# An encoder layer on one core: another sequence of the softmax work, the first norm summed by ScalarE, and a split first load

## The chip, the cores and the metric

The kernel runs on one core of a Trainium2 chip. The metric is the device time of one execution in microseconds (us); the kernel before has a median of 1122.74 us over 3 runs (1122.15 to 1123.06). Profiles and traces are of one execution each. Engines are named PE (TensorE's matrix multiply), PEld (its weight loads, which overlap PE), DVE (VectorE), ACT (ScalarE), POOL (GpSimd) and SP (SyncE, which only issues DMAs here).

## The reference, cut to what matters

One layer over 1024 tokens of width 1024, in float32. What the change touches is the first norm, the input projection and the attention:

```
hn = rmsnorm(h, norm_mix_g[i])
z = hn @ w_in[i]                       # 512 pooling columns, then q, k, v (8 heads of 64)
...
s = jnp.einsum('bqhd,bkhd->bhqk', qb, kb) * scale + bias     # scale 1/8
s = jnp.where(valid[None, None, None, :], s, -jnp.inf)
pr = jax.nn.softmax(s, axis=-1)
return jnp.einsum('bhqk,bkhd->bqhd', pr, vb)
```

Each chunk of 64 queries attends to its own chunk and the 8 before. A pooling mixer, an output projection, a gated MLP with a short convolution, a gated embedding and a last norm follow; the change leaves them alone.

## The kernel before, in words

**Arithmetic.** Every float32 operand of a product is split in two halves of PE's faster float type, hi (a copy, on ACT) and lo (the difference, on DVE). A product is three matmuls: hi by hi, hi by lo, lo by hi (`mm3`, lines 136 to 138). `split` (lines 141 and 142) is the general splitter.

**Start.** Activations lie transposed: rows of `xT` are channels, eight tiles `k` of 128 channels by 1024 tokens. For each `k`, SP's queue brings `xT[k]` in two halves, a tile of `w_v`, and blocks of the first q/k weights `w_qk0`; ACT's queue brings `vecs`, all the per-channel vectors in one, whose first 8 columns are the first norm's. ACT and DVE make hi and lo of x times the norm's vector (lines 248 and 249) and of the weights. PE runs `start_mm(k)` (12 matmuls) and `start_v(k-1)` (9 matmuls). Ahead of all that, 8 matmuls on zeros (line 221) keep PE busy while the first loads come. The norm's 1/rms is applied after the products. For it, `squared(k)` squares `xraw[k]` on ACT (line 227, in place) and adds it to a running sum on DVE (line 229); eight products with a column of ones (line 264) sum over the 128 channels of a tile's rows; DVE and POOL make `rstd_tok` (lines 265 and 266). `rstd_rows` turns it by PE into rows (line 323), between the first `start_v` tiles and the later ones.

**Attention.** A unit is a pair of heads `c` and one or three token tiles (`UNITS`: per pair `(0,1,2)`, then 3, 4, 5, 6, 7; `PER` is 6 and `NU` is 24). `unit(u)` writes for PE: the transposes of the last unit's probabilities (`probs_t`, line 421), this unit's scores (`scores`, line 398), and some steps of the projections still to be made (`fill`, three matmuls a step). At the ends of three groups of tiles, (0,1,2), (3,4,5) and (6,7), `values` (line 473) multiplies the probabilities of the whole group with V. That makes 12 value groups in all, three to each head pair.

The order of PE's work is the program's. In the attention ACT's and DVE's order is written by hand too: each piece of work is pushed with a time in `push(t, ...)`, and `flush()` emits all that is pending, sorted by that time. The pieces of a unit:

- `softmax`: `least` (a fused add and minimum on DVE, lines 363 and 367), the exponentials with their sums (ACT, line 375), the reciprocals (DVE, line 378), and the scaling of the first head of the pair on DVE (line 373) and of the second on ACT (line 371). Scores carry a minus sign: q is scaled by -0.125, and the bias is turned by ACT (`load_bias`, line 351), while POOL writes the masked corners (lines 352 and 353).
- `probs_out`: the transposed probabilities go from PSUM to hi (ACT, line 439) and lo (DVE, line 441). What lies in the banks behind 3 ("far") has later times than the rest ("near"). `values` reads both.
- `lay` (lines 308 to 312) and `split_later` (lines 502 and 504): the halves of q and k for a later unit, and of weights for a later projection. `qk_out` (line 279) and the projection of the pooling columns (line 559) move finished projections out of PSUM.

In `unit`, all that is pending is emitted ahead of the value products. `values` itself ends with two ACT copies into `otmp` (line 476) and two DVE additions (line 479).

Outside the attention a scheduler with a cost model of its own orders ACT, DVE, POOL and the DMA issues; a queue's DMAs are issued one after another.

Of the kernel before, what the change touches and what calls it, by code (L numbers as in the profile page):

```python
# [8 lines left out]
AF = mybir.ActivationFunctionType  # L9
# [89 lines left out]
    return t1 * t + k if t0 == 0 else 5 * (t - t0) + k - t + 4 - max(0, 4 - t0)  # L99


def trunk(tc, xT, pT, vecs, w_qk0, w_in, w_v, bias, counts, pool_w, w_out, w_up, w_down,
          w_gate, w_ple, out):
    nc = tc.nc
    act, dve, pe, pool, sp = nc.scalar, nc.vector, nc.tensor, nc.gpsimd, nc.sync
# [1 line left out]
    with tc.tile_pool(name="sb", bufs=1) as sb, \  # L107
# [42 lines left out]
        pool.memset(ident, 0.0)  # L150
        pool.affine_select(out=ident, in_=ident, compare_op=ALU.not_equal, fill=1.0, base=0,
                           pattern=[[-1, P]], channel_multiplier=1)
        act.activation(small[:, 1:2], mhalf, AF.Exp)
        rstd_tok = small[:, 8:16]
        st = [small[:, b:b + 3] for b in (24, 27, 30, 33, 56, 59, 62, 66)]
        cnt = small[:, 40:56]

# [47 lines left out]
            return PS[:, (4, 5, 6, 4, 5, 6, 7, 3)[t]]  # L205

        def start_mm(k):
            for h in range(2):
                for c in range(2):
                    mm3(PS[:, 2 * c + h], w0h[:, k, c * P:(c + 1) * P], w0l[:, k, c * P:(c + 1) * P],  # L210
                        XTH[h][:, k], XTL[h][:, k], k == 0, k == KT - 1)
# [10 lines left out]

        blocks = {(0, 0): (0, 1), (0, 1): (1, 2), (1, 1): (2, 4), (3, 1): (4, 8)}

        def squared(k):

            act.activation(xraw[k], xraw[k], AF.Square)
            if k:
                dve.tensor_tensor(xraw[0], xraw[0], xraw[k], ALU.add)

        def split_v(k):
            split(wvraw[k % 4], wv[0][:, k], wv[1][:, k])
# [1 line left out]
        for k in range(KT):  # L234
            xs = xraw[k]
            for h in range(2):
                sp.dma_start(xs[:, h * 512:(h + 1) * 512], xT[k, :, h * 512:(h + 1) * 512])
                if k == 0 and h == 0:
                    act.dma_start(vec, vecs)
                if h and k:  # L240
                    sp.dma_start(wvraw[(k - 1) % 4], w_v[:, (k - 1) * 512:k * 512])
                if (k, h) in blocks:
                    ka, ke = blocks[k, h]
                    sp.dma_start(wq[:, ka:ke], w_qk0[:, ka * 256:ke * 256].rearrange("p (k c) -> p k c", c=256))
            g = vec[:, C_GMIX + k:C_GMIX + k + 1]
            for h in range(2):
                xk = xs[:, h * 512:(h + 1) * 512]
                act.activation(XTH[h][:, k], xk, AF.Copy, scale=g)
                dve.scalar_tensor_tensor(XTL[h][:, k], xk, g, rv(XTH[h][:, k]), ALU.mult, ALU.subtract)  # L249
                if h == 0:  # L250
                    split(wq[:, k], w0h[:, k], w0l[:, k])
            if k:
                split_v(k - 1)
                squared(k - 1)
            if k < KT - 1:
                start_mm(k)
            if k:
                start_v(k - 1)
        sp.dma_start(wvraw[(KT - 1) % 4], w_v[:, (KT - 1) * 512:])
        split_v(KT - 1)  # L260
        squared(KT - 1)
        sp.dma_start(cnt, counts)
        for t in range(NTOK):
            pe.matmul(PS[:, 7, t:t + 1], xraw[0][:, t * P:(t + 1) * P], ones, start=True, stop=True)
        dve.tensor_scalar(rstd_tok, PS[:, 7, 0:NTOK], 1.0 / D, EPS, ALU.mult, ALU.add)
        pool.tensor_tensor(rstd_tok, rstd_tok, mhalf.to_broadcast([P, NTOK]), ALU.pow)
        start_mm(KT - 1)
        start_v(KT - 1)
# [12 lines left out]
        laid = set()  # L281
        pending, now, owed = [], [0.0], set()

        def push(t, *fns):

            for n, fn in enumerate(fns):
                pending.append((t + 0.8 * n, len(pending), fn))

        def flush():
            todo = sorted(pending, key=lambda p: p[:2])  # L290
            pending.clear()
            owed.clear()
            for _, _, fn in todo:
                fn()


        def lay(c, x, h):

            z = slice(h * 512, (h + 1) * 512)

            def last(fn):
                fn()
                laid.add((c, x, h))

            src = qk32[x][:, z]
            if x:
# [39 lines left out]
        def load_bias(h):  # L346
            b = biasb[h % 3]
            sp.dma_start(b, bias[h])

            def turned():  # L350
                act.activation(b, b, AF.Copy, scale=-1.0)
                pool.memset(b[0:64, 576:640], BIG)
                pool.memset(b[64:128, 0:64], BIG)
            return turned

        def softmax(todo, valued):

            for i, (x, b, ps, S, s_) in enumerate(todo):
                z = 2 * i / len(todo)

                def least(b=b, ps=ps, S=S, s_=s_):
                    if len(ps.shape) == 3:
                        dve.tensor_tensor_reduce(  # L363
                            S.rearrange("p (a b) -> p a b", a=2), ps,
                            b.rearrange("p (a b) -> p a b", a=2), 1.0, BIG, ALU.add, ALU.min, s_[:, 0:1])
                    else:
                        dve.tensor_tensor_reduce(S, ps, b, 1.0, BIG, ALU.add, ALU.min, s_[:, 0:1])
# [7 lines left out]
                push(1.9 + 0.85 * z, lambda S=S, s_=s_: act.activation(  # L375
                    S, S, AF.Exp, bias=s_[:, 0:1], scale=-1.0, accum_out=s_[:, 1:2]))
# [57 lines left out]
        def probs_out(todo, valued):  # L434
            for a, b, bank, ps in todo:
                src = ps.rearrange("p a (n q) -> p n a q", q=HD)
                hi, lo = [pt[:, a:b].rearrange("p k x (a q) -> p (k x) a q", a=2) for pt in PT]
                far = bank > 3
                push(3.5 if far else 0.0, lambda hi=hi, src=src: act.activation(hi, src, AF.Copy))
                push((3.55 if valued else 4.4) if far else 2.5 if valued else 3.7,  # L440
                     lambda lo=lo, src=src, hi=hi: dve.tensor_tensor(lo, src, rv(hi), ALU.subtract))

        credit, turns, valued = 0.0, [], [False]
# [1 line left out]
        def values(u):  # L445
# [6 lines left out]
            while u < NU - 1 and at[0] < 2.3:  # L452
                next(fill)
                credit -= 0.5
                now[0] += STEP
            flush()
            reach = {k: (max(t0, k), min(t1, k + BANDT)) for k in range(max(0, t0 - 4), t1)}
            wide = [k for k, (a, b) in reach.items() if b - a == n]
            narrow = sorted((k for k in reach if k not in wide), key=lambda k: reach[k][1] - reach[k][0])
# [13 lines left out]
                    pe.matmul(Os[j][:, (a - t0) * P:(b - t0) * P].rearrange("p (t q) -> p t q", q=P), V[:, k, 2 * c_ + j],  # L473
                              PT[part][:, b0:b0 + by * (b - a - 1) + 1:by, j], start=n_ == 0, stop=n_ == len(todo) - 1)
# [22 lines left out]
        def split_later(parts):  # L497

            t = max(5.2, now[0] + 0.4)
            for i, (name, src, hi, lo) in enumerate(parts):  # L500
                def low(name=name, src=src, hi=hi, lo=lo):
                    (pool if name[0] in (4 + 1, 8 + 2, 4 + 2, 8 + 3, 2) else dve).tensor_tensor(lo, src, rv(hi), ALU.subtract)
                    there.add(name)
                push(t + 0.7 * i, lambda src=src, hi=hi: act.activation(hi, src, AF.Copy))
                push(t + 0.8 + 0.7 * i, low)

        def weights(ct, half):

# [138 lines left out]
        def lay_due(u):  # L647

            for c, x, h in list(qk_ready):
                if u >= (c - 1) * PER + (0 if x else PER - 1 if h else 1):  # L650
                    qk_ready.remove((c, x, h))
                    push(max(4.8, now[0] + 0.4), *lay(c, x, h))

        for h in range(3):
            load_bias(h)()
# [1 line left out]
        def unit(u):  # L657
# [758 lines left out]
def _layout(i):  # L1416
# [49 lines left out]
```

## Time and profile before

| what | value |
|---|---|
| median of 3 runs | 1122.74 us (1122.15 to 1123.06) |
| profiled execution | 1122.08 us |
| its span (first to last instruction) | 1120.3 us |
| PE busy | 1108.7 us, 5674 matmuls |
| PEld busy | 921.3 us |
| DVE busy | 850.7 us |
| ACT busy | 581.7 us |
| POOL busy | 167.9 us |
| HBM traffic | 109.13 MB read, 14.68 MB written |

Busy time of an engine is the time that at least one of its instructions was running. Matmuls are pipelined: a 128x512 matmul is shown with 0.39 us, but the next one starts 0.23 us after it, so starts are compared with starts. A row of the timeline gives start, length, engine, line, operation, what is written and read, shape, and the number of instructions merged; the bracket at its end is the engine's idle time just before, and what ended it.

### The profile page before, as it was taken

The page shows a single profiled execution, that of the slowest core. Times are in us where ns is not written, and L with a number is a line of the kernel's source. Part 1 is how long each engine was busy: PE and PEld are TensorE (multiplying, and loading weights), DVE is VectorE, ACT ScalarE, POOL GpSimd, SP SyncE. Part 2 cuts the span into 40 slices and gives each one's busy share as a digit, 9 for nine tenths or more (in the row PEclk, how much of TensorE's full clock was granted, in tenths as well). Part 3 has the DMA queues.
Part 4 walks back from the last instruction along what each step waited for, and adds up shares of the span by engine and source line. Part 5 has one row for each costly group of instructions (what it writes and reads, how often), then busy time and mean ns, then how long its engine had stood idle before and what let it go on. Part 6 is the DMA issues. An engine that isn't in the chain of part 4 may idle for free.

```text
span 1120.3 us, 15614 instructions
## 1 busy us (share of the span) xinstructions
PE 1108.7 (99%) x5674; PEld 921.3 (82%) x5674; DVE 850.7 (76%) x1438; ACT 581.7 (52%) x1006; POOL 167.9 (15%) x212
## 2 busy tenths in 40 slices
PE   9999999999999999999999999999999999999997
PEld 7888888888888888888888888888888888888887
DVE  7537777778578878887787878777877789986845
ACT  8336777765665545443443444344544444674634
POOL 0000101186013200220121012201120112000000
PEclk9999999999999999999999999999999999999999
DMA  8100111104600452764567456756575556420003
GB/s 308 50 1 20 62 43 39 51 16 136 197 29 1 109 155 95 164 156 140 150 160 168 133 160 151 172 138 160 142 174 145 137 156 140 132 94 20 1 34 117
DMA packets 64878, 124.83 MB, mean 111 GB/s; under 512 B 7329, under 2 KB 8737, under 8 KB 64801
## 3 DMA queue, kind: packets, MB, share of 16 engines
q1 hardware_dynamic: 50688, 98.33, 26.8%
q0 software_dynamic: 13824, 25.17, 14.2%
q8 instruction: 44, 0.72, 0.3%
q10 hardware_dynamic: 288, 0.33, 0.1%
q14 instruction: 34, 0.27, 0.1%
HBM read 109.13 MB, written 14.68 MB: 111 GB/s over the span
## 4 chain that ended last, share of the span: by engine, by line
PE 65%; DVE 3%; issue 2%; ACT 1%; POOL 1%; POOLq 0%; DVEq 0%; ACTq 0%
PE PS L136 21%; PE PS L137 21%; PE PS L138 21%; DVE R L142 1%; ACT R L141 1%; POOL TB L925 0%; POOL F L915 0%; DVE F L907 0%; DVE F L1191 0%; ACT TB L896 0%; PE PS L778 0%; POOL small L782 0%; ACT F L770 0%; DVE TB L918 0%; DVE TB L919 0%
## 5 line engine op out<-in xcount | busy, mean ns | idle before, releaser
L136 PE MATMUL PS<-R 128*128 128x512 f32 (+1 forms) x1088 | 422.2, 388 | 0.2
L137 PE MATMUL PS<-R 128*128 128x512 f32 (+1 forms) x1088 | 418.7, 385 | 0.0
L138 PE MATMUL PS<-R 128*128 128x512 f32 (+1 forms) x1088 | 418.5, 385 | 0.0
L136 PEld LDWEIGHTS PS<-R 128*128 128x128 f32 x1088 | 204.6, 188 | 44.6 <-issue 2.9
L138 PEld LDWEIGHTS PS<-R 128*128 128x128 f32 x1088 | 204.5, 188 | 41.3
L137 PEld LDWEIGHTS PS<-R 128*128 128x128 f32 x1088 | 204.6, 188 | 39.8 <-DVE R L249 0.2
L141 ACT ACTIVATE R<-F 128x512 fp32r<-128x512 f32 (+2 forms) x221 | 137.4, 636 | 177.1 <-PE PS L137 85.6
L142 DVE TENSOR_TENSOR R<-F,R 128x512 fp32r<-128x512 f32 (+2 forms) x221 | 154.5, 713 | 49.7 <-ACT R L141 49.0
L1160 DVE TENSOR_TENSOR F<-F,PS 128x512 f32<-128x512 f32 x140 | 92.6, 681 | 6.8 <-PE PS L138 6.5
L850 DVE TENSOR_TENSOR F<-F 128x512 f32<-128x512 f32 x88 | 60.5, 688 | 44.8 <-DMA F<-in_w_up 42.1
L141 ACT ACTIVATE BQ<-RW 128x512 fp32r<-128x512 f32 x90 | 52.6, 622 | 80.4 <-PE PS L137 76.3
L1103 POOL DMA_DIRECT2D RW<-Yd x56 | 49.5, 889 | 264.4 <-DMA RW<-Yd 200.8
L1103 POOL DMA_DIRECT2D RW<-in_w_down x40 | 36.5, 966 | 228.7 <-DMA RW<-in_w_down 191.1
L142 DVE TENSOR_TENSOR BQ<-RW,BQ 128x512 fp32r<-128x512 f32 x90 | 59.1, 684 | 2.6 <-PE PS L137 2.2
L137 PE MATMUL PS<-BQ 128*128 128x512 f32 x140 | 54.6, 390 | 0.1
L136 PE MATMUL PS<-R,BQ 128*128 128x512 f32 x140 | 54.5, 389 | 0.0
L138 PE MATMUL PS<-R,BQ 128*128 128x512 f32 x140 | 54.5, 389 | 0.0
L136 PE MATMUL PS<-BQ 128*128 128x512 f32 x140 | 54.5, 389 | 0.0
L137 PE MATMUL PS<-R,BQ 128*128 128x512 f32 x140 | 54.5, 389 | 0.0
L138 PE MATMUL PS<-BQ 128*128 128x512 f32 x140 | 54.5, 389 | 0.0
L986 ACT ACTIVATE F<-F,vec 128x1024 f32<-128x1024 f32 (+1 forms) x25 | 28.6, 1143 | 44.1 <-DVE F L961 41.9
L375 ACT ACTIVATE F<-F,small 128x640 f32<-128x640 f32 (+4 forms) x64 | 44.0, 689 | 14.0 <-DVE small L363 12.6
(177 smaller groups left out, 1589.7 us busy)
## 6 DMA issues: line engine op xcount, KB each, us to landing
F<-in_w_up SPq DMA_DIRECT2D x91, 256.0 KB, 4.3
RW<-Yd SPq DMA_DIRECT2D x60, 256.0 KB, 3.8
RW<-Yd POOLq DMA_DIRECT2D x56, 256.0 KB, 4.9
RW<-in_w_down SPq DMA_DIRECT2D x50, 256.0 KB, 2.9
RW<-in_w_down POOLq DMA_DIRECT2D x40, 256.0 KB, 6.6
Yd<-F SPq DMA_DIRECT2D x40, 256.0 KB, 3.1
F<-in_w_in SPq DMA_DIRECT2D x10, 512.0 KB, 3.5
F<-in_xT SPq DMA_DIRECT2D x16, 256.0 KB, 5.4
```

Source lines behind the costliest of these rows:

```text
L136: pe.matmul(ps, ahi, bhi, start=first, stop=False, skip_group_check=more)
L137: pe.matmul(ps, ahi, blo, start=False, stop=False, skip_group_check=more)
L138: pe.matmul(ps, alo, bhi, start=False, stop=last, skip_group_check=more)
L141: both = (act.activation(hi, src, AF.Copy), dve.tensor_tensor(lo, src, rv(hi), ALU.subtract))
L142: dve.tensor_tensor(lo, src, rv(hi), ALU.subtract))
L375: push(1.9 + 0.85 * z, lambda S=S, s_=s_: act.activation(S, S, AF.Exp, bias=s_[:, 0:1], scale=-1.0, accum_out=s_[:, 1:2]))
L850: return dve.tensor_tensor(rawu[to], rawu[a], rawu[b], op)
L986: act.activation(y, Gb[:, 2 + a:2 + b], AF.Identity, bias=vec[:, C_CB + fi:C_CB + fi + 1], scale=cw(2))
L1103: pool.dma_start(t, src, accum_op=ALU.add)
L1160: dve.tensor_tensor(t, t, PS[:, 4 + d], ALU.subtract if n in (1, 5) else ALU.add)
```

## The change

- **Order of the attention's work.** `push` takes a mark `slow`, which `lay_due` and `split_later` set. Ahead of a value group only what is not slow is emitted, then the value products; the slow pieces are emitted after the first half's copy and addition (groups of three tiles), or after both (the group of two). The copies and additions at the end of `values` now alternate. In `probs_out`, the far hi copy has time 0.05 in place of 3.5, and the far lo difference directly follows the near one, which has 3.55 in place of 3.7 where no value group follows.
- **Sign of the scores.** q is scaled by +0.125; `least` multiplies by -1 in the same instruction. ACT's turning of the bias goes; the two masked corners are written by DVE with -BIG in place of POOL with BIG.
- **The norm's sums.** A second copy of the input, `xn`, lies token by token. Its eight tiles of 128 tokens by 1024 channels (512 KB each) are loaded by SP into the `xraw` buffers after use, the first four inside the loop over `k`, the others after it. ACT squares each in two halves and sums along the row in the same instruction (`accum_out`). The running sum on DVE and the eight products with ones on PE go.
- **The first loads.** ACT's queue brings only the first norm's 8 columns of `vecs`, then the second half of `xT[0]`; then comes the `Exp` that had stood at the top of ACT's stream. The rest of `vecs` follows on SP's queue. The hi of the first q/k weight tile is a DVE copy in place of ACT's, and `start_mm(0)` has another order: per half of the tokens, hi by hi for both weight columns, then lo by hi, then hi by lo.

```diff
-        act.activation(small[:, 1:2], mhalf, AF.Exp)
...
+            if k == 0:
+                for h in range(2):
+                    for i, (w_, x_) in enumerate(((w0h, XTH), (w0l, XTH), (w0h, XTL))):
+                        for c in range(2):
+                            pe.matmul(PS[:, 2 * c + h], w_[:, 0, c * P:(c + 1) * P], x_[h][:, 0], start=i == 0, stop=False)
+                return
...
-            act.activation(xraw[k], xraw[k], AF.Square)
-            if k:
-                dve.tensor_tensor(xraw[0], xraw[0], xraw[k], ALU.add)
+            for h, s in enumerate((rstd_tok, ssq2)):
+                half = xraw[t][:, 512 * h:512 * (h + 1)]
+                act.activation(half, half, AF.Square, accum_out=s[:, t:t + 1])
+
+        def load_tokens(t):
+            sp.dma_start(xraw[t], xn[t])
...
-                    act.dma_start(vec, vecs)
+                    act.dma_start(vec[:, 0:C_CW], vecs[:, 0:C_CW])
+                    act.dma_start(xs[:, 512:1024], xT[0, :, 512:1024])
+                    act.activation(small[:, 1:2], mhalf, AF.Exp)
+                if (k, h) == (1, 1):
+                    sp.dma_start(vec[:, C_CW:], vecs[:, C_CW:])
...
+                if h == 0 and k == 0:
+                    dve.tensor_copy(w0h[:, 0], wq[:, 0])
+                    dve.tensor_tensor(w0l[:, 0], wq[:, 0], rv(w0h[:, 0]), ALU.subtract)
...
-                squared(k - 1)
+            if k > 3:
+                load_tokens(k - 4)
+            if k > 4:
+                squared(k - 5)
...
-        squared(KT - 1)
+        for t in range(4, NTOK):
+            load_tokens(t)
+        for t in range(3, NTOK):
+            squared(t)
         sp.dma_start(cnt, counts)
-        for t in range(NTOK):
-            pe.matmul(PS[:, 7, t:t + 1], xraw[0][:, t * P:(t + 1) * P], ones, start=True, stop=True)
-        dve.tensor_scalar(rstd_tok, PS[:, 7, 0:NTOK], 1.0 / D, EPS, ALU.mult, ALU.add)
+        dve.tensor_tensor(rstd_tok, rstd_tok, ssq2, ALU.add)
+        dve.tensor_scalar(rstd_tok, rstd_tok, 1.0 / D, EPS, ALU.mult, ALU.add)
...
-        def flush():
-            todo = sorted(pending, key=lambda p: p[:2])
-            pending.clear()
+        def flush(part=False):
+            todo = sorted((p for p in pending if not (part and p[3])), key=lambda p: p[:2])
+            pending[:] = [p for p in pending if part and p[3]]
...
-            return [lambda: act.activation(hi, src, AF.Copy, scale=-0.125),
-                    lambda: last(lambda: dve.scalar_tensor_tensor(lo, src, -0.125, rv(hi), ALU.mult, ALU.subtract))]
+            return [lambda: act.activation(hi, src, AF.Copy, scale=0.125),
+                    lambda: last(lambda: dve.scalar_tensor_tensor(lo, src, 0.125, rv(hi), ALU.mult, ALU.subtract))]
...
-                act.activation(b, b, AF.Copy, scale=-1.0)
-                pool.memset(b[0:64, 576:640], BIG)
-                pool.memset(b[64:128, 0:64], BIG)
+                dve.memset(b[0:64, 576:640], -BIG)
+                dve.memset(b[64:128, 0:64], -BIG)
...
-                        dve.tensor_tensor_reduce(S, ps, b, 1.0, BIG, ALU.add, ALU.min, s_[:, 0:1])
+                        dve.tensor_tensor_reduce(S, ps, b, -1.0, BIG, ALU.add, ALU.min, s_[:, 0:1])
...
-                push(3.5 if far else 0.0, lambda hi=hi, src=src: act.activation(hi, src, AF.Copy))
-                push((3.55 if valued else 4.4) if far else 2.5 if valued else 3.7,
+                push(0.05 if far else 0.0, lambda hi=hi, src=src: act.activation(hi, src, AF.Copy))
+                push((2.5 if valued else 3.55) + 0.02 * far,
...
-            flush()
+            flush(True)
...
-                act.activation(otmp[halves[j], 0:n * P], Os[j][halves[1 - j]], AF.Copy)
-            for j in range(2):
                 a = halves[j]
-                dve.tensor_tensor(o32[a, c_, t0 * P:t1 * P], Os[j][a], otmp[a, 0:n * P], ALU.add)
+                act.activation(otmp[a, 0:n * P], Os[j][halves[1 - j]], AF.Copy)
+                if n == 2 and j == 0:
+                    continue
+                for i in range(2) if n == 2 else (j,):
+                    a = halves[i]
+                    dve.tensor_tensor(o32[a, c_, t0 * P:t1 * P], Os[i][a], otmp[a, 0:n * P], ALU.add)
+                if j == 0:
+                    flush()
...
+            if valued[0]:
+                flush(True)
+                values(u - 1)
             flush()
-            if u:
-                values(u - 1)
...
+    d["xn"] = c(x).reshape(NTOK, P, D)
```

More of the change, by code (lines that the diff above doesn't have):

```diff
@@ L99, in block_at, with trunk @@
     return t1 * t + k if t0 == 0 else 5 * (t - t0) + k - t + 4 - max(0, 4 - t0)
-def trunk(tc, xT, pT, vecs, w_qk0, w_in, w_v, bias, counts, pool_w, w_out, w_up, w_down,
+def trunk(tc, xT, xn, pT, vecs, w_qk0, w_in, w_v, bias, counts, pool_w, w_out, w_up, w_down,
           w_gate, w_ple, out):
@@ L152, in trunk @@
                            pattern=[[-1, P]], channel_multiplier=1)
-        act.activation(small[:, 1:2], mhalf, AF.Exp)
-        rstd_tok = small[:, 8:16]
+        rstd_tok, ssq2 = small[:, 8:16], small[:, 56:64]
         st = [small[:, b:b + 3] for b in (24, 27, 30, 33, 56, 59, 62, 66)]
@@ L223, in trunk, with squared @@
         blocks = {(0, 0): (0, 1), (0, 1): (1, 2), (1, 1): (2, 4), (3, 1): (4, 8)}
-        def squared(k):
-            act.activation(xraw[k], xraw[k], AF.Square)
-            if k:
-                dve.tensor_tensor(xraw[0], xraw[0], xraw[k], ALU.add)
+        def squared(t):
+            for h, s in enumerate((rstd_tok, ssq2)):
[3 more added lines that the diff above has]
+            sp.dma_start(xraw[t], xn[t])
         def split_v(k):
@@ L236, in trunk @@
             for h in range(2):
-                sp.dma_start(xs[:, h * 512:(h + 1) * 512], xT[k, :, h * 512:(h + 1) * 512])
+                if (k, h) != (0, 1):
+                    sp.dma_start(xs[:, h * 512:(h + 1) * 512], xT[k, :, h * 512:(h + 1) * 512])
                 if k == 0 and h == 0:
-                    act.dma_start(vec, vecs)
+                    act.dma_start(vec[:, 0:C_CW], vecs[:, 0:C_CW])
[3 more added lines that the diff above has]
+                    sp.dma_start(vec[:, C_CW:], vecs[:, C_CW:])
                 if h and k:
@@ L249, in trunk @@
                 dve.scalar_tensor_tensor(XTL[h][:, k], xk, g, rv(XTH[h][:, k]), ALU.mult, ALU.subtract)
-                if h == 0:
+                if h == 0 and k == 0:
+                    dve.tensor_copy(w0h[:, 0], wq[:, 0])
+                    dve.tensor_tensor(w0l[:, 0], wq[:, 0], rv(w0h[:, 0]), ALU.subtract)
+                elif h == 0:
                     split(wq[:, k], w0h[:, k], w0l[:, k])
@@ L282, in trunk, with push @@
         pending, now, owed = [], [0.0], set()
-        def push(t, *fns):
+        def push(t, *fns, slow=False):
             for n, fn in enumerate(fns):
-                pending.append((t + 0.8 * n, len(pending), fn))
-        def flush():
-            todo = sorted(pending, key=lambda p: p[:2])
-            pending.clear()
+                pending.append((t + 0.8 * n, len(pending), fn, slow))
+        def flush(part=False):
+            todo = sorted((p for p in pending if not (part and p[3])), key=lambda p: p[:2])
+            pending[:] = [p for p in pending if part and p[3]]
             owed.clear()
-            for _, _, fn in todo:
-                fn()
+            for p in todo:
+                p[2]()
         def lay(c, x, h):
@@ L364, in least @@
                             S.rearrange("p (a b) -> p a b", a=2), ps,
-                            b.rearrange("p (a b) -> p a b", a=2), 1.0, BIG, ALU.add, ALU.min, s_[:, 0:1])
+                            b.rearrange("p (a b) -> p a b", a=2), -1.0, BIG, ALU.add, ALU.min, s_[:, 0:1])
                     else:
-                        dve.tensor_tensor_reduce(S, ps, b, 1.0, BIG, ALU.add, ALU.min, s_[:, 0:1])
+                        dve.tensor_tensor_reduce(S, ps, b, -1.0, BIG, ALU.add, ALU.min, s_[:, 0:1])
                 def scaled(x=x, S=S, s_=s_):
@@ L503, in low @@
                     there.add(name)
-                push(t + 0.7 * i, lambda src=src, hi=hi: act.activation(hi, src, AF.Copy))
-                push(t + 0.8 + 0.7 * i, low)
+                push(t + 0.7 * i, lambda src=src, hi=hi: act.activation(hi, src, AF.Copy), slow=True)
+                push(t + 0.8 + 0.7 * i, low, slow=True)
         def weights(ct, half):
@@ L651, in lay_due @@
                     qk_ready.remove((c, x, h))
-                    push(max(4.8, now[0] + 0.4), *lay(c, x, h))
+                    push(max(4.8, now[0] + 0.4), *lay(c, x, h), slow=True)
         for h in range(3):
```

## The prediction

> **What bounds the kernel now.** I read the page first, then PE's waits, then PE's timeline around them, then the other engines there.
>
> ```profile
> span 1120.3 us, 15614 instructions
> PE 1108.7 (99%) x5674; PEld 921.3 (82%) x5674; DVE 850.7 (76%) x1438; ACT 581.7 (52%) x1006; POOL 167.9 (15%) x212
> ```
> PE is the bound. An edit pays where it removes PE instructions or a stall of PE, and nowhere else. PE's waits from 44 to 330 us, the stretch that holds the attention:
>
> ```profile
> PE PS L473 <- DVE B L441: 1.8, 4, 0.8
> PE PS L421 <- DVE B L441: 0.8, 2, 0.5
> PE PS L473 <- ACT B L439: 0.5, 1, 0.5
> ```
> Columns: waiter and awaited; total, times, longest. All seven waits are for hi (439) or lo (441) of the probabilities. Idle time understates them, since a busy PE may be draining, so I compare equal stretches. PE's timeline, value products (473) and transposes (421):
>
> ```profile
> 104.06 1.33 PE L473 MATMUL PS<-B,R 128*128 128x384 f32 x7
> 105.68 2.70 PE L473 MATMUL PS<-B,R 128*128 128x128 f32 x17 [0.29 <-DVE B L441]
> ...
> 119.92 0.51 PE L473 MATMUL PS<-B,R 128*128 128x256 f32 x3
> 120.97 0.96 PE L473 MATMUL PS<-B,R 128*128 128x128 f32 x6 [0.55 <-ACT B L439]
> 122.39 2.02 PE L473 MATMUL PS<-B,R 128*128 128x128 f32 x15 [0.46 <-DVE B L441]
> ...
> 149.07 3.66 PE L473 MATMUL PS<-B,R 128*128 128x384 f32 x24
> ...
> 159.04 0.92 PE L421 MATMUL PS<-ident,F 64*128 64x64 f32 x20 [0.33 <-DVE B L441]
> ...
> 166.78 2.96 PE L473 MATMUL PS<-B,R 128*128 128x256 f32 x24
> ...
> 176.90 1.79 PE L473 MATMUL PS<-B,R 128*128 128x384 f32 x12
> ...
> 219.18 0.73 PE L473 MATMUL PS<-B,R 128*128 128x384 f32 x4
> 220.67 1.31 PE L473 MATMUL PS<-B,R 128*128 128x128 f32 x8 [0.76 <-DVE B L441]
> ...
> 249.65 0.59 PE L421 MATMUL PS<-ident,F 64*128 64x64 f32 x12 [0.46 <-DVE B L441]
> ```
> Group (3,4,5): 104.06 to 108.38 is 4.32 us, its twin at 149.07 takes 3.66, so the stall costs 0.66. The first row of waits has four, 1.8 us in all; less 0.29, 0.46 and 0.76 a fourth of 0.29 is left, a like group: 0.66 again. Group (6,7): 119.92 to 124.41 is 4.49 against 2.96: 1.53. Group (0,1,2): 219.18 to 221.98 is 2.80 against 1.79: 1.01. For the two stalled transposes I take the idle time, 0.33 and 0.46. Together 2 x 0.66 + 1.53 + 1.01 + 0.79 = 4.65 us. That is all the order of ACT and DVE can return.
>
> **The change, part 1: the order in the attention.** What was late in each stall:
>
> ```profile
> 105.20 0.42 DVE L441 TENSOR_TENSOR B<-PS,B 128x256 fp32r<-128x256 f32 x1
> ...
> 117.64 0.29 DVE L367 CUSTOM_DVE_ANT_0 F<-PS,F 128x128 f32<-128x128 f32 x1 [1.07 <-POOL F L352]
> ...
> 157.19 0.67 DVE L279 TENSOR_TENSOR F<-PS,F 128x512 f32<-128x512 f32 x1
> 157.77 1.54 DVE L441 TENSOR_TENSOR B<-PS,B 128x1024 fp32r<-128x1024 f32 x2
> ```
> The far lo stood behind reciprocals and a scaling; now it directly follows the near lo. At 105.20 the near one (1.21 us, as the 183.02 row below) had been done since about 104.6, so the far one ends near 105.0, and the eighth product, free at about 105.2 (104.06 + 1.33 less a drain), finds it. That stall and its like go. At 119.92 the far hi, behind six exponentials, released PE at 120.97, and the far lo at 122.39. With time 0.05 the far hi precedes the exponentials. Also `least` no longer waits 1.07 us for POOL's corner, since DVE writes it in its own order; near lo (1.21) and far lo (0.42) then end some 2.2 us sooner, near 120.1, while hi products still occupy PE. Both stalls go. At 157.19 an evacuation due at 3.6 stood ahead of a near lo due at 3.7, and before 249.65 one stood ahead of a far lo due at 4.4; 3.55 and 3.57 now precede them, and PE gets its bank 0.67 us sooner, more than 0.33 and 0.46. The evacuations come up to 1.54 us later; no PE row waits on line 279 or 559, so I price that at nothing. At 219 the far lo moves ahead of a scaling: gone too.
>
> What the change adds: the deferred halves (`lay`, weights) now run between the two `otmp` copies, ahead of the next unit's `least`.
>
> ```profile
> 176.92 0.62 ACT L504 ACTIVATE R<-F 128x512 fp32r<-128x512 f32 x1
> ...
> 180.31 0.82 DVE L363 CUSTOM_DVE_ANT_0 F<-PS,F 128x640 f32<-128x640 f32 x1 [0.50 <-PE PS L398]
> ...
> 183.02 1.21 DVE L441 TENSOR_TENSOR B<-PS,B 128x1024 fp32r<-128x1024 f32 x1
> ...
> 184.51 0.84 PE L421 MATMUL PS<-ident,F 64*128 64x64 f32 x20
> ```
> This is the fullest group, (0,1,2) of the third pair: three deferred ACT copies of 0.62 us, and DVE differences after them. They now stand between the copies of the two halves, 1.86 us in a place where PE's second half (0.9, half of 1.79) had ACT idle for perhaps 0.4: the second addition comes 1.4 later. Less the 0.50 idle ahead of `least`, plus two corners of 0.1 (estimate: a quarter of the 0.42 for 128x256), `least` starts 1.1 later, at 181.4. The near lo ends at 185.3 in place of 184.2, and the transposes, which came at 184.51, wait 0.8. The like group of the second pair has two deferred copies and gets perhaps 0.1. In the group of two the deferred work follows both copies and delays the next unit's start by a copy, 0.6; that eats perhaps 0.3 of the return at 219, where the scaling is now last. I take 1.2 us lost. Bounds: 0, if ACT's and DVE's idle time swallows it; 2.2, if four groups lose 0.55. Part 1 nets 4.65 - 1.2 = 3.45 (2.4 to 4.65).
>
> ACT also loses eight turnings of the bias and DVE gains 16 corners: both engines have idle time around (0.50 in the `least` row), so beyond the stalls named nothing.
>
> **Part 2: the sums of the first norm.** PE loses the products with ones.
>
> ```profile
> 39.37 1.84 PE L264 MATMUL PS<-small,F 128*128 128x1 f32 x16
> 41.07 0.49 PE L136 MATMUL PS<-R 128*128 128x512 f32 x1
> ...
> L227 ACT ACTIVATE F<-F 128x1024 f32<-128x1024 f32 x8 | 8.4, 1046 | 0.0
> L375 ACT ACTIVATION_READ_ACCUMULATOR F<-F,small 128x1 f32 x64 | 12.0, 187 | 0.0
> 10.00:20.00 10.00, 10.00 (x46) 8.23 (x45) 9.99 (x17) 10.00 (x18) 0.00 (x0) 1.00 1.04 391
> 19.92 0.33 SPq L259 DMA_DIRECT2D F<-in_w_v  x1
> F<-in_w_v SPq DMA_DIRECT2D x8, 256.0 KB, 5.5
> 41.57 1.67 POOL L266 TENSOR_TENSOR small<-small 128x8 f32<-128x8 f32 x1 [5.54 <-DVE small L265]
> 45.98 0.60 PE L323 MATMUL PS<-ident,small 128*128 128x128 f32 x4
> ```
> 41.07 - 39.37 = 1.70 us leave PE's stream, which is full there: a certain gain. What it costs lies beside PE. DVE loses seven additions; ACT's 8.4 us become 16 halves of 0.523 + 0.187 = 11.4 us. SP's queue gains 4.19 MB while the window row shows 16 full DMA engines (share 1.04) at 391 GB/s: 10.7 us more of transfers. The last weight tile, issued at 19.92, lands about 25.4, so the last tokens land by about 36.1. Two halves (1.4), two DVE steps on 128x8 (0.4 at most, the price of 128x256) and POOL's 1.67 follow: `rstd_tok` by about 39.7. PE's turning into rows needs it at 45.98, now 2.0 sooner, at 44.0; the spare is 4 us. The products with ones had no other user. x and the weights behind the token tiles (up to three tiles, 4 us, before `xT[7]`) are used far later than they land: `xT[7]` only from 41.07, now 39.1. Bias and projection weights behind them come 11 us later, for use after 70 us. So nothing.
>
> **Part 3: the first loads.**
>
> ```profile
> 1.49 3.78 PE L221 MATMUL PS<-B 128*128 128x512 f32 x8 [1.49 <-DVE B L219]
> 5.31 0.80 PE L136 MATMUL PS<-R 128*128 128x512 f32 x1
> ...
> 6.68 0.39 PE L136 MATMUL PS<-R 128*128 128x512 f32 x1
> ...
> 4.23 0.72 ACT L248 ACTIVATE R<-F,vec 128x512 fp32r<-128x512 f32 x1 [1.56 <-DMA vec<-in_vecs]
> vec<-in_vecs ACTq DMA_DIRECT2D x1, 68.0 KB, 3.5
> small<-in_counts SPq DMA_DIRECT2D x1, 8.0 KB, 4.4
> ```
> ACT's queue issues the small vector and x's second half while ACT idles (1.56 us in the 4.23 row); the rest of `vecs`, 64 KB, costs SP's stream 0.2 us at 391 GB/s ahead of the first `w_v` tile, whose products come only after the 24 of `start_mm(0)` and `start_mm(1)`. The eight zero matmuls end at 5.27, and the first real one starts at 5.31: little can be won before it. Behind it three starts are late for their operands, 5.31 to 6.68 where full rate would take 3 x 0.23; at most 0.7 us. The new order asks for the lo halves later, but these matmuls also run slowly: eight in 3.78 us is (3.78 - 0.80) / 7 = 0.43 a step against 0.23 after 6.68. Four at 0.43 from 5.1 put the fifth near 6.8, against 6.91 now. I take 0.3. Bounds: 0.7 gained if the rate is full from 5.3, 0.9 lost if the small first vector lands as late as the small `counts` does (4.4 against 3.5).
>
> [...]
>
> **Sum.** 3.45 + 1.70 + 0.3 = 5.45 us. The profiled execution's 1122.08 (span 1120.3 and 1.8 around it) becomes 1116.6; it stands 0.66 below the median, from which the sum gives 1117.3. I say 1117.0. Behind 250 us PE has no wait in its view, so an earlier start moves everything up.
>
> **The rivals.**
> - *The wait moves to the transposes* (chance 0.18): what the far lo and the deferred work push back, scaling and the next near lo, becomes what PE waits for in most groups. For: the 184.51 calculation. Against: the scaling has a whole value group (1.8 to 3.7 us) before it is read. Then half of Part 1's net: 5.45 - 1.7 = 3.7, 1119.0.
> - *The deferred halves delay `least` everywhere; slower* (0.07): the place is the unit after each of the 12 value groups, the price up to one 0.62 copy and one 0.69 difference, 1.3 us. It decides when the mean loss passes (4.65 + 2.0) / 12 = 0.55 us; at 0.8 the time is 1122.7 + 2.9 = 1125.6. Against: only the fullest groups have more than one deferred copy.
> - *The norm comes late* (0.08): if ACT or SP put the bias and weights first, `rstd_tok` comes past 44.0 and PE idles. Each us beyond costs one; past 5.45 the change is no gain. With 4 us: 1121.
> - *The start gains nothing, the clock's doing* (0.05): half rate past 6.7 us hides the operands' lateness; the sum without the 0.3 is 1117.3. [...]
>
> **How the numbers follow.** The forecast, with most stalls gone and one or two small new ones, has 0.62. A measurement here tells 0.2%, 2.2 us, from no change. The forecast, the last rival and the first are faster: 0.85; of these I leave 0.03 to gains below 2.2. Same: that 0.03 and most of the late norm, 0.09. Slower: the second rival and the worst of the third, 0.09. The range: below, all of Part 1 and 0.7 from Part 3 give 7.05, 1115.0 from the profiled execution; above, the first rival with Part 1 at its low bound and 0.9 lost at the start, 1122.7 - 2.4 / 2 - 1.7 + 0.9 = 1120.7. Outside lie the slower rival, half of the late norm, and a few hundredths of the forecast.
>
> **What would show it.** Line 264 gone from PE and 1.7 us with it. In PE's waits the three rows gone or under 1 us, and the value groups at 1.8, 3.0 and 3.7 us each. A wait of some 0.7 us at the transposes after the third pair's first group. The fifth real matmul near 6.7. POOL's power ending before 40, and PE not waiting for it. I am wrong if PE waits anew on the scalings (371, 373), on a deferred half, or at the rows of `rstd_tok`.

## The result, and the profile after: 6 us slower

The changed kernel has a median of 1128.51 us (1126.68 to 1130.56), the kernel before on the same chip 1122.16: ratio 1.0054, 95% interval 1.0041 to 1.0067. The forecast was 1117.0, faster. The profiled execution took 1126.68 us. Head of its page:

```profile
span 1124.9 us, 15599 instructions
PE 1109.0 (99%) x5658; PEld 919.9 (82%) x5658; DVE 842.8 (75%) x1449; ACT 579.9 (52%) x1021; POOL 163.5 (15%) x196
```

The profiled execution is the fastest of the six; it is 4.6 us longer than that of before (1122.08), so of the 6 us some 1.4 lie outside what this trace shows.

PE issues 16 matmuls fewer and is busy no shorter. PE's waits from 44 to 330 us, in the form of the three rows of before (transposes are now line 441, scores 418, value products 493, hi 459, lo 461, pushed weights 529 and 527):

```profile
PE PS L441 <- DVE B L461: 3.9, 7, 0.8
PE PS L136 <- ACT B L529: 1.5, 1, 1.5
PE PS L493 <- ACT F L391: 0.9, 1, 0.9
PE PS L138 <- DVE B L527: 0.3, 1, 0.3
PE PS L493 <- DVE B L461: 0.2, 1, 0.2
```

The value products' waits for hi and lo are down from 2.3 us to 0.2. That is idle time, which understates a stall: the first row below shows none and is 0.44 us longer than the second. By the lengths of the twelve value groups, the prediction's own measure, less is gained: together they take 37.7 us before and 36.2 here (sums of such rows). Two rows for the first pair's group (3,4,5), the first from after, the second from kernel e10 below, where nothing holds it up:

```profile
102.62 4.09 PE L493 MATMUL PS<-B,R 128*128 128x384 f32 x24
```
```profile
101.98 3.65 PE L493 MATMUL PS<-B,R 128*128 128x384 f32 x24
```

It took 4.32 before (prediction). So stalls of the value products remain, and the transposes now wait seven times for the lo (3.9 us). PE also waits for pieces of weights at lines 136 and 138, where it waited for nothing. The wait of 0.9 is put down to ACT's scaling (391, in the group at 167.02). The evacuation in line 300 ended 0.05 us before that scaling, and in e1 and e5 the same place waits for line 300, so the trace leaves open which of the two PE needed.

PE's timeline dates the loss; with the rows of before at 41.07, 184.51 and 220.67 (prediction) each start gives a shift:

```profile
38.58 0.39 PE L136 MATMUL PS<-R 128*128 128x512 f32 x1
...
97.98 0.92 PE L441 MATMUL PS<-ident,F 64*128 64x64 f32 x20 [0.62 <-DVE B L461]
...
143.09 0.92 PE L441 MATMUL PS<-ident,F 64*128 64x64 f32 x20 [0.84 <-DVE B L461]
...
185.73 0.83 PE L441 MATMUL PS<-ident,F 64*128 64x64 f32 x20 [0.83 <-DVE B L461]
...
221.86 1.68 PE L493 MATMUL PS<-B,R 128*128 128x128 f32 x8 [0.16 <-DVE B L461]
...
263.30 0.50 PE L136 MATMUL PS<-R,B 128*128 128x512 f32 x1 [1.51 <-ACT B L529]
...
264.35 0.50 PE L138 MATMUL PS<-R,B 128*128 128x512 f32 x1 [0.32 <-DVE B L527]
```

38.58 against 41.07: the start gained 2.5 us in this trace (part of that is the clock, see Part 3 below). 185.73 against 184.51 and 221.86 against 220.67: by then the attention has given back 3.7. The same matmul as at 263.30 started at 259.24 before: the last 2.9 us go between 221 and 263. From there on nothing changes (4.7 late at the end). So the whole loss of this trace lies in the attention.

What made the lo late is in DVE's waits, 72 to 262 us, after:

```profile
DVE F L502 <- ACT F L497: 19.8, 17, 4.0
DVE F L383 <- ACT B L459: 19.6, 16, 3.0
```

The first row, the additions behind the `otmp` copies, was 19.0 us before and is little changed. `least` (363 before, 383 now) waits 16 times for ACT's hi copy, 19.6 us. The same stretch of before has `least` wait for the scores:

```profile
DVE F L363 <- PE PS L398: 12.2, 13, 2.3
```

In the timeline of after, ACT, then DVE, in one unit:

```profile
137.80 1.28 ACT L459 ACTIVATE B<-PS 128x1024 fp32r<-128x1024 f32 x2
...
139.12 0.82 DVE L383 CUSTOM_DVE_ANT_0 F<-PS,F 128x640 f32<-128x640 f32 x1 [1.01 <-ACT B L459]
```

The two hi copies, near and far, end at 139.08, and `least` starts 0.04 behind them, having idled 1.01 us. In the same unit of before, `least` ran beside the near copy:

```profile
139.24 1.01 ACT L439 ACTIVATE B<-PS 128x1024 fp32r<-128x1024 f32 x1
```
```profile
139.63 0.82 DVE L363 CUSTOM_DVE_ANT_0 F<-PS,F 128x640 f32<-128x640 f32 x1
```

So it is the far copy that holds `least`. By the code, the scores lie in banks 4 to 7 of PSUM (the memory for PE's results), and the far probabilities in the last columns of banks 6 and 7; the near ones lie in 2 and 3. So `least` and the far copy read the same two banks, in other columns, and neither uses what the other makes. With time 0.05 the far copy comes first in the program, and in the rows of after `least` starts only when it is done (139.12 against 139.08). What makes it wait no run shows; the traces show the waits and that they follow the program's order. With the copy second, in kernel e1 below, it is ACT's copy that waits, three times, for a `least` (line 387):

```profile
ACT B L459 <- DVE small L387: 2.9, 3, 1.0
```

### The profile page after: what moved, and what is told of

It reads as the page before. It is cut to its first block, busy times and chain, and to the rows that moved or that the text cites. A ratio compares the mean times of both kernels' runs of the same rounds, so it can differ in the third digit from the quotient of the medians.

```text
span 1124.9 us, 15599 instructions
## 1 busy us (share of the span) xinstructions
PE 1109.0 (99%) x5658; PEld 919.9 (82%) x5658; DVE 842.8 (75%) x1449; ACT 579.9 (52%) x1021; POOL 163.5 (15%) x196
## 4 chain that ended last, share of the span: by engine, by line
PE 84%; DVE 7%; ACT 5%; issue 3%; POOL 1%; POOLq 0%; DVEq 0%; ACTq 0%
PE PS L136 26%; PE PS L137 26%; PE PS L138 26%; PE PS L493 3%; ACT F L395 2%; DVE B L461 2%; ACT B L459 1%; DVE F L383 1%; DVE R L142 1%; PE PS L441 1%; PE PS L418 1%; ACT R L141 0%; POOL TB L951 0%; POOL F L941 0%; ACT F L497 0%
```

## The experiments

Two theories. **A**: the far hi copy, now ahead of `least` on the same banks, delays `least`, the exponentials and the near lo in the units that have a far part. **B**: the deferred pieces (`slow`) do it. Each kernel's ratio is to the kernel before on the same chip; us in the text are ratio differences times 1122.5. The 95% interval of a ratio is 1 to 2 us to either side, and a difference of two is uncertain by as much.

**e1, undo A.** After, with

```diff
-                push(0.05 if far else 0.0, lambda hi=hi, ...
+                push(2.4 if far else 0.0, lambda hi=hi, ...
```

> The kernel after, with one number changed: the far hi copy has time 2.4 in place of 0.05, so that ACT's copy is emitted after both `least` of its unit, and still ahead of the far lo. Theory A (readers of one PSUM bank are ordered: `least` reads banks that the far hi copy reads too, and with the copy emitted first it waits for ACT): the 19.6 us that line 383 waited for ACT's line 459 in the kernel after go, and the transposes no longer wait for the near lo in units without deferred work; some 5 us come back, about 1123.5 from 1128.5. Theory B (the deferred halves make the loss): no more than 1 us changes, 1127.5 to 1129.

1123.28 us, ratio 1.0003 (0.9994 to 1.0012): 5.7 us of the loss gone, as A said. PE's waits:

```profile
PE PS L136 <- ACT B L529: 1.5, 1, 1.5
PE PS L441 <- DVE B L461: 1.2, 2, 0.8
PE PS L493 <- DVE F L300: 0.9, 1, 0.9
PE PS L138 <- DVE B L527: 0.3, 1, 0.3
```

The transposes' waits fall from 3.9 to 1.2; what B names (529, 527) stays. On DVE, 72 to 262 us, the 19.6 us that `least` waited for ACT's copy are gone, and it waits for the scores again:

```profile
DVE F L383 <- PE PS L418: 10.2, 9, 2.2
```

**e2, A alone.** Before, with far hi at 0.05 in place of 3.5 and nothing else.

> The kernel before, with one number changed: the far hi copy has time 0.05 in place of 3.5, nothing else of the change. Theory A: `least` starts behind ACT's copy in every unit with a far part, 0.7 to 0.9 us later, and PE waits at the transposes: 4 to 6 us slower than before, 1126 to 1128. Theory B: nothing lost, and the stall of 1.5 us at the first group of two partly gone: 1121 to 1122.5.

1129.66, ratio 1.0067 (1.005 to 1.0084): 7.5 us lost by one number, more than the 4 to 6 expected. DVE's waits, 72 to 262 us, and PE's, 44 to 330:

```profile
DVE F L363 <- ACT B L439: 19.8, 16, 3.1
```
```profile
PE PS L473 <- DVE B L441: 4.6, 7, 1.5
PE PS L421 <- DVE B L441: 2.4, 4, 0.7
```

The same 16 waits on DVE, and PE's waits go from 3.1 us to 7.0. A is shown from both sides.

**e3, undo B.** After, all pieces again emitted at one flush ahead of the value products:

```diff
-            if valued[0]:
-                flush(True)
-                values(u - 1)
             flush()
+            if u:
+                values(u - 1)
...
-            flush(True)
+            flush()
```

> The kernel after, without the deferral: all that is pending is emitted ahead of the value products, as before; the far hi copy keeps its early time. Theory A: the losses of the units with deferred work go (2.2 us at the first projection matmul after the last value products, 1.0 and 0.5 at the transposes after the first groups of the third and second pair), the rest stays: about 1124.5. Theory B: most of the loss goes, 1119 to 1121.

1123.81, ratio 1.0014 (1.0004 to 1.0023): 4.5 us of the loss gone, while `least` still waits 16 times for ACT's copy (19.9 us). So A is not the only cause.

**e5, undo both.**

> The changed kernel with the far hi copy at time 2.4 (behind the least of its unit) and without the deferral (every pushed piece runs at the first flush, values ahead of it as before). Theory A (same-bank order holds least up) and theory B (deferred halves) are separate causes: their shares 5.2 and 4.7 us add, 1128.5 - 9.9 = 1118.6, which is 1.4 below the kernel with the start alone (1120.0); that 1.4 is then what the rest of the attention's part (near lo ahead of evacuations, DVE's corners) is worth. Rival: both put off the same chain (least, exponentials, near lo), so that either one alone leaves it just off PE's path; then undoing the second adds little, 1122 to 1123.

1119.37, ratio 0.9971 (0.996 to 0.9982): 9.3 us faster than after, where the two separate shares add to 10.2. They are separate causes, and the rival (either alone suffices) falls. PE's remaining waits:

```profile
PE PS L493 <- DVE F L300: 0.9, 1, 0.9
PE PS L418 <- DVE F L502: 0.9, 2, 0.5
```

**e7, B alone**: before, with the deferral and the alternating copies only.

> The kernel before with only the deferral and the alternating otmp copies and additions of the value groups; far hi stays at 3.5, the start and the signs as before. Theory B: 1125.5 to 1127.5, 3 to 5 us slower than before, 1.8 to 2.2 of it a wait of PE behind the last value products, for the last unit's weight halves (ACT and DVE). Theory A as the only cause: the same as before, 1122 to 1123.

1127.82, ratio 1.0045 (1.003 to 1.006): 5.0 us lost. **e8, B without the last unit**: after, with

```diff
-                flush(True)
+                flush(u < NU)
```

> The changed kernel, with the deferral left out in the last unit only. Theory B at its largest single place: the 1.5 us wait for ACT's weight half and the 0.3 to 0.5 us for DVE's behind it are gone, 1.8 to 2.2 us; if the drop of the granted clock that followed that wait in one profile also comes often, another 0 to 1.7: 1124.6 to 1126.7, with a narrower spread than 1126.7 to 1130.6. If the wait only moves to another operand of those matmuls: 1128, as changed.

1125.28, ratio 1.0025 (1.0014 to 1.0035): 3.3 us better than after; the waits for 529 and 527 are gone from its list and nothing comes in their place. So 3.3 of B's 4.5 us lie in this one place. The timeline of after, ACT and then DVE, shows why:

```profile
261.82 0.77 ACT L497 ACTIVATE F<-PS 64x256 f32<-64x256 f32 x2 [3.03 <-PE PS L493]
262.62 0.63 ACT L529 ACTIVATE B<-F 128x512 fp32r<-128x512 f32 x1
```
```profile
263.51 0.78 DVE L527 TENSOR_TENSOR B<-F,B 128x512 fp32r<-128x512 f32 x1
```

After the last group PE's next work is a projection with that weight, not another unit's transposes. Before, the same difference ran ahead of the last value products:

```profile
255.35 0.68 DVE L502 TENSOR_TENSOR B<-F,B 128x512 fp32r<-128x512 f32 x1
```

Deferred, it stands behind them, while ACT idles 3.03 us. The rest of B is in the groups of three tiles, as in e7's timeline, ACT and then DVE:

```profile
223.54 0.49 ACT L477 ACTIVATE F<-PS 64x384 f32<-64x384 f32 x1 [1.37 <-PE PS L473]
223.93 0.62 ACT L509 ACTIVATE R<-F 128x512 fp32r<-128x512 f32 x1
224.57 0.48 ACT L477 ACTIVATE F<-PS 64x384 f32<-64x384 f32 x1
```
```profile
224.06 0.55 DVE L482 TENSOR_TENSOR F<-PS,F 64x384 f32<-64x384 f32 x1 [1.11 <-ACT F L477]
224.58 1.02 DVE L507 TENSOR_TENSOR R<-F,R 128x512 fp32r<-128x512 f32 x1
225.63 0.56 DVE L482 TENSOR_TENSOR F<-PS,F 64x384 f32<-64x384 f32 x1
```

ACT idles 1.37 us for the products, and then does the weight between the two copies; the second addition, which frees the bank, starts at 225.63, where without the weight's copy on ACT and its difference on DVE it could follow the first at about 224.6 (an estimate: 224.06 + 0.55).

**e4 and e12, the start.** Before with parts 2 and 3 alone (e4), and with the norm's sums alone (e12).

> The kernel before with the two start parts of the change alone: the norm's sums on ScalarE from token tiles, and the first loads with the new order of the first matmuls. Sequence and sign of the attention are those of before. Both theories place the loss in the attention, so this one keeps what the trace of the kernel after shows ahead of it: PE reaches the first scores 2.6 us sooner, 1119.5. If the start were part of the loss (its DMAs or its later weights), 1122 or more.

> The kernel before with the norm's sums alone (token tiles, squares summed by ACT, no products with ones); first loads as before. The prediction's step: 1.70 us of PE's stream gone, nothing waits: 1121.1, ratio 0.9985. With the measured gain of sums and first loads together, 2.5, the first loads are then worth 0.8. Rival: the norm's row products come to wait; then a wait of PE for POOL shows near 44 us, and the gain is smaller.

e4: 1120.01, ratio 0.9978 (0.9969 to 0.9988), 2.5 us gained; e12: 1120.94, ratio 0.9985 (0.9976 to 0.9994), 1.7 us, which leaves 0.8 for the first loads. e12's list of PE's waits is that of before, row for row.

**e6, far hi behind the exponentials where a unit has six `least`.** Both undone, and there far hi 3.4, far lo 3.45.

> As the kernel with both undone, but in the units of three token tiles, which have six least, the far hi has time 3.4 and the far lo 3.45; elsewhere 2.4 and 2.52. Theory A: where there are six least, a far hi at 2.4 still stands in ACT's queue ahead of two or three exponentials and waits there for the last least of its bank; putting it behind them takes away the wait of the value products for the evacuation (0.9 us once with the far hi at 2.4): 0.5 to 1.5 us faster than with both undone. If the far hi's place past the last least does not matter: the same within 0.4.

1119.27, ratio 0.997 (0.9958 to 0.9981): the same as e5, and the wait of the value products for the evacuation (line 300) stays at 0.9. So that the far hi stands ahead of some exponentials is not the cause of this wait.

**e9 to e11**, each with both undone and one thing more: corners by POOL and ACT as before (e9); near lo at 3.7 again where no value group follows (e10); the second weight halves sooner (e11).

> As the kernel with both undone (1119.4, ratio 0.9971 to the kernel before), but the bias is again turned by ACT and its corners are written by POOL. The prediction's step: DVE's corners take POOL's 1.07 us out of least's way, and cost nothing else; then this is up to 1 us slower than with both undone, and the product group of two stalls again (ratio about 0.998). Rival: DVE's two corners (0.11 us each, 0.3 with their gaps, right ahead of least) cost as much as POOL's did: the same within 0.4, and the 0.9 us wait of the value products for the evacuation shrinks to about 0.6.

> As the kernel with both undone, but in the units without value products of a group the near lo has time 3.7 again, behind an evacuation due at 3.6. The prediction's step: the evacuation behind the near lo costs nothing, and the near lo behind the evacuation costs 0.33 to 0.79; then 0.3 to 0.8 us slower. Rival: the later evacuation delays the laid halves, the next least and so the next evacuation, which held the value products for 0.9 us once; then that wait goes, and this is the same or up to 0.6 faster.

> As the kernel with both undone, but ACT's copy of a weight tile's second half has time 3.85 or the time of its request, ahead of the scalings (ACT waits there for reciprocals, 1.2 us in one case), where it had 5.2 or later, ahead of the copies of the value products. If the scores' two waits of 0.4 to 0.5 us come from that copy standing ahead of the otmp copies: they go, 0.5 to 1.2 us faster (about 1118.4). If the copy then delays ACT's scaling, or the halves are not the ones in the way: the same within 0.4.

e9: 1119.35, ratio 0.9969 (0.9958 to 0.9981): who writes the corners makes no difference that can be measured. e11: 1119.31, ratio 0.9967 (0.9955 to 0.998): no difference either, and it decides little, because in its trace the copies at the two places of the scores' waits had not moved.

e10: 1117.98, ratio 0.9957 (0.9945 to 0.997), the lowest of all: its highest run, 1118.78, is under the lowest of e9 on the same chip, 1118.86. The rival of the expectation was right about the direction; the gain, 1.3 to 1.6 us against e9, e11 and e5, is more than its 0.6. e5's timeline, DVE and then ACT:

```profile
154.92 1.54 DVE L461 TENSOR_TENSOR B<-PS,B 128x1024 fp32r<-128x1024 f32 x2
156.37 0.68 DVE L300 TENSOR_TENSOR F<-PS,F 128x512 f32<-128x512 f32 x1
157.75 0.69 DVE L333 SCALAR_TENSOR_TENSOR R<-F,R 128x512 fp32r<-128x512 f32 x1 [0.70 <-ACT R L332]
```
```profile
157.09 0.63 ACT L332 ACTIVATE R<-F 128x512 fp32r<-128x512 f32 x1 [1.22 <-DVE F L300]
```

The evacuation (300) behind the near lo makes ACT wait 1.22 us for it in `lay`, and DVE then 0.70 for ACT; that comes off the next unit's `least`, and at that unit's end an evacuation again is late for the value products (it starts at 164.19 in e5 and at 162.78 in e10; 0.6 of the difference comes from the start of the kernel). In e10:

```profile
154.89 1.54 DVE L461 TENSOR_TENSOR B<-PS,B 128x1024 fp32r<-128x1024 f32 x2
156.35 0.68 DVE L333 SCALAR_TENSOR_TENSOR R<-F,R 128x512 fp32r<-128x512 f32 x1
```

Line 333 follows at once, and PE's list has no wait for line 300 left:

```profile
PE PS L418 <- DVE F L502: 0.9, 2, 0.5
PE PS L441 <- DVE B L461: 0.6, 1, 0.6
```

e10 is the change without three of its steps. It beats both kernels, and the median forecast for the whole change, 1117.0, lies 1.0 below it.

## Why the prediction was wrong, step by step

By the runs: start -2.5; the attention's other edits -2.4 (e10 against e4); near lo ahead of the evacuation +1.6 (e10 to e5); far hi early +5.7 (e1); deferral +4.5 (e3). That sums to +6.9; the last two overlap by 0.9 (e5), which leaves the measured +6.0. The small shares (1.6, and the overlap of 0.9) are no larger than their uncertainty.

- **The step that failed most: "With time 0.05 the far hi precedes the exponentials."** I counted what the far hi gains on ACT and not what it is moved past: `least`, on DVE, which reads the same banks. Price 5.7 us (7.5 in e2, alone), given as nothing. Neither the sum nor a rival had it. The first rival named the place, the transposes, but by scalings and deferred work and at 1119.0; the slower rival had `least` late everywhere, but by the deferred pieces, and at 1125.6.
- **Deferral: 1.2 us lost, 2.2 at most; measured 4.5 (e3) and 5.0 (e7).** For the third pair's first group the place and size were right: a wait of 0.8 was forecast at 184.51, and the transposes there wait 0.83, in after and in e1 alike (0.8, the longest of its two). What was missed is the last unit, 3.3 us by e8. I priced the group of two as delaying "the next unit's start", and the last group has no next unit: PE needs the deferred weight there at once. The 1.2 us that are left of the 4.5 equal the forecast, but only one of its places was compared with a row, so part of that may be luck. A wait of PE on a deferred half, which the prediction named as a sign that it is wrong, is in after's list (529 and 527).
- **"The evacuations come up to 1.54 us later; no PE row waits on line 279 or 559, so I price that at nothing."** Wrong by 1.6 us. Line 279 was off PE's list because it came in time; behind it stand `lay`, the next `least` and the next evacuation. The 0.33 and 0.46 that the step was to gain were worth less than that.
- **The stalls of 4.65 us** went only in part in after (36.2 us for the value groups against 37.7): groups forecast at 1.8, 3.0 and 3.7 us still reach 4.09 there, and the group (0,1,2) at 220.74 takes 2.80 as before. With A and B undone they do go: in e10 every group takes 1.79, 2.96 or 3.65 to 3.67 us, 33.6 together, 4.1 less than before. But a PE that comes sooner meets the next wait: e10 still has the scores wait twice for the `otmp` additions (0.9) and a transpose (0.6), and the net is 2.4.
- **Corners**: priced at nothing beyond POOL's 1.07, which stood in a stall that goes anyway; e9 finds no difference.
- **Part 2** was right: 1.70 forecast, 1.7 in e12. POOL's power was forecast by 39.7; in after:

```profile
36.47 1.66 POOL L287 TENSOR_TENSOR small<-small 128x8 f32<-128x8 f32 x1 [0.94 <-DVE small L286]
```

- **Part 3**: 0.3 forecast, bounds 0.7 and -0.9; the difference of e4 and e12 is 0.8, with an uncertainty as large. The traces do not settle it either. e12, with the old loads, reaches the first scores at 72.04 us, and the ten kernels with the new loads at 71.67 to 72.85, after first of all. In the traces' record of the granted clock full speed begins at 4.74 us in e12 and at 4.55 (after) to 7.69 (e1) in the ten; in before it is 6.51, with steps of 0.43 us ahead of it and of 0.23 behind. So the moment at which the clock came up moved the start by as much as the new loads were to bring. The rival's half rate past 6.7 us was met in e1's trace at least; what sets the moment no run shows.

## What to carry to other kernels

Moving an instruction earlier on one engine can delay another engine that reads none of its data (here `least`, 16 waits of 19.6 us in all, behind a copy from other columns of two of its PSUM banks): ask which PSUM banks both touch, and in which order the program then names them. A piece that "nobody waits for" must be followed through the pieces that it feeds until one of them reaches the bounding engine, and every loop has a last turn in which the next consumer is another. Here work in an idle time ahead of a wait cost nothing, and the same work right behind the wait did: for the last unit's weight halves PE waited 1.51 and 0.32 us in after, and not at all in before.

## What the hardware showed beyond that

In two profiles short waits of PE were followed by a slower clock. In e1's the waits of 1.51 and 0.29 us that ended at 258.68 and 259.70 were followed by a granted clock of half. Windows: length, then busy time of PE, PEld, DVE, ACT and POOL, the granted clock, DMA share, GB/s:

```profile
258.00:260.00 2.00, 1.03 (x3) 0.60 (x4) 1.59 (x3) 0.63 (x1) 1.84 (x3) 1.00 0.00 0
260.00:264.00 4.00, 4.00 (x12) 3.12 (x11) 1.12 (x2) 1.78 (x4) 3.61 (x7) 0.57 0.19 66
```

and in e7's it came after the wait of 1.19 us that ended at 223.00:

```profile
222.00:224.00 2.00, 0.99 (x8) 1.00 (x8) 0.95 (x2) 0.63 (x3) 1.76 (x4) 1.00 0.00 0
224.00:226.00 2.00, 2.00 (x27) 1.87 (x27) 1.91 (x3) 1.78 (x4) 1.84 (x3) 0.62 0.00 0
226.00:227.00 1.00, 1.00 (x9) 0.67 (x5) 0.24 (x2) 0.28 (x1) 0.84 (x3) 0.50 0.35 57
227.00:228.00 1.00, 1.00 (x3) 0.81 (x4) 1.00 (x3) 0.18 (x1) 0.92 (x2) 0.56 0.61 205
```

A mean of 0.57 over 4 us is half speed for 3.4 us; 0.62, 0.50 and 0.56 in the other three windows also make 3.4 us (1.52 + 1.00 + 0.88). The traces' record of the granted clock has one such stretch in each of the two, 3.41 us long. At half speed that is 1.7 us lost: in e1's timeline a 128x512 matmul starts 0.43 us after the one before it there (260.68 to 261.11), and 0.23 behind the stretch (263.92 to 264.15). The same waits in after's profile (1.51 and 0.32) left the clock full, and e7's own at 264.78 (1.51) did too, so it depends on more than the wait's length; on what, no run shows.

The mean granted clock of each timed run tells how often it happened. Of e1's ten runs four have 0.998 or 0.999 and take 1120.28 to 1121.61 us; six have 0.996 or 0.997 and take 1123.19 to 1124.47. Of e7's four, two at 0.998 take 1127.06 and 1127.11, two at 0.996 take 1128.53 and 1128.66. So e1's median holds this loss. Its four runs at full clock alone would put A at some 7.4 us, close to the 7.5 of e2, and the overlap of A and B would then be larger. After has three runs at 0.996 or 0.997, but its three at 0.998 have a median of 1128.18, so the clock does not explain its loss, nor what e8's 3.3 us hold beyond the two waits (1.83): that stays open.
